# Moving token forms, attention steps, output transposes and a load in a two-layer trunk kernel

## The chip, the cores and the metric

The kernel runs on one core of a Trainium2 chip. The metric is the device time of one execution in microseconds, as the median of several executions. The profile is one further execution, taken by the hardware profiler; its times are in microseconds from the first instruction (the span). TensorE is called PE in it, VectorE DVE, ScalarE ACT, GpSimd POOL and SyncE SP.

## The reference, cut to what matters

One step of a trunk of two layers over 128 prompt tokens and 512 sample tokens (640 in all), width 2048, all in float32. Each layer normalises its input and modulates it with a scale and a shift, projects it, mixes, and projects back with a gated residual:

```
h  = rms_norm(x, g) * (1 + scale) + shift
layer 0:  mixers A (windowed attention) and B (gated short convolution)
layer 1:  cq, ck, cv, cg, dq, dk, dv, dg = split(h @ w_in)
          C: o = softmax(q1 k1) v - lambda * softmax(q2 k2) v, rms_norm per head, 4 heads, v of 256
          D: dense grouped-query attention, 8 heads on 2 keys
          out = concat(C * silu(cg), D * silu(dg)) @ w_out
x = x + gate * out
```

The keys and values of 256 cached tokens are put ahead of the sample's own. Outputs are the new x of both groups and the new keys and values.

## The kernel before, in words

**Layout.** The activations are held transposed: channels on the 128 partitions, the 640 tokens along the free dimension, in two halves of 320 (`HV`). A tile is 128 columns of a weight matrix times all 640 tokens. Every operand is split into a high and a low part (`split`, L212: ScalarE copies to the rounded type, L213, VectorE subtracts, L214), and a product is three matmuls: high by high, high by low, low by high (L248 to L250, and L510 to L512 for pairs).

**Tiles in `run_tiles` (L292).** A tile has 16 blocks of the contraction in four quarters; a quarter (`proj_q`, L241) does four blocks for each half, 24 matmuls. So a tile is 32 groups of three matmuls, 96 in all. The first tiles of a run are leading tiles: they go together, quarter by quarter, while `make_h` makes the activations that they need. Afterwards tiles go one at a time; weights are loaded five quarters and split three quarters ahead.

**Two queues of work beside the tiles.** `prep` holds what a finished tile still needs (a key's normalisation and rotation, for example), `attn` holds attention steps, or the making of token forms. Both are Python generators; a step is what lies between two yields. `slot` (L284) advances all of `prep` and one step of `attn`; it is called after each quarter. With `mid` (layer 1's attention stage only) a fifth step is taken between the two halves of the second quarter (L384 to L387). `release` (L269) advances attention until nothing in it still reads a tile that is about to be given away. The order of the lines is the order in which the work is asked for; the framework's scheduler places each engine's instructions by it and by when it takes them to be ready, and gives out buffers as they come free.

**Pairs in `run_pairs` (L419).** Two output tiles at once are computed by seven products of half the contraction and half the tokens instead of eight: `Q1`, `N5`, `P6`, `Q2`, `P7`, `Q3`, `P4`. Some use sums of weight blocks: N5 uses A21 + A22 (L450), P6 adds A11 (L453), Q2 uses A12. A11, A12 and A21 are loads of 512 KB into four buffers named `w8`; A22 is two ordinary quarters. Before the first pair they are asked for in the order A11, A12, A21, A22 (L498). There are three such starts: layer 0's output projection, layer 1's first input columns, layer 1's output projection.

**Forms.** The products also need sums of token blocks, the forms T: `make_form` (L1055) computes three sums and a difference of 320 columns each on VectorE (L1057 to L1060) and splits the 960 columns. In layer 1 `forms1` (L1297) makes eight of them from the modulated x (`x1`), which it first finishes on ScalarE (L1306). It is put on `attn` when `h1_maker` (L1268) makes block 8 (L1294); the blocks come in the order 0 to 3, 8 to 11, 4 to 7, 12 to 15 in the leading tiles, of which there are three. Form j waits until block j + 8 is made. `project` (L1111) runs the leading tiles, then the single tiles up to the sixth, then the pairs; it advances `attn` once after each leading tile's quarter and twice per quarter in the single tiles.

**Layer 1's attention stage.** For each head of C four tiles are projected: two queries and two keys. `k_gen` (L553) turns a key tile: it copies it out, transposes it, normalises and rotates it, yields twice, releases the old key, and transposes it back. With the second key the value comes and then attention: `diff_gen` (L1403) goes through five blocks of 128 queries in `score` (two score matrices into one buffer S, softmax), `groups` (transposes of the probabilities), `weigh` (times v, L1437 to L1439, then the norm over ACT, DVE, POOL and DVE, L1441 to L1448) and `out` (two transposes, L1454, and the gate). Each block's parts lie in successive steps: `out(u - 2)` and `score(u, 0)` and `groups(u - 1)` in one, `score(u, 1)` and `weigh(u - 1)` in the next. D's heads use `pair_gen` in the same manner.

Of the kernel before, what the change touches and what calls it, by code (L numbers as in the profile page):

```python
# [50 lines left out]
def trunk_kernel(ctx: ExitStack, tc: tile.TileContext, I: dict, O: dict):  # L51
# [189 lines left out]
    def proj_q(pp, part, qd, pos, halves=HV, alone=False, js=(0, 4)):  # L241
        wh, wl = part
        for half_i, sl in halves:
            ps = pp[half_i][:, 0:HALF]
            for j in range(*js):
# [3 lines left out]
                PE.matmul(ps, wh[:, i, :], lo[:, sl], start=False, stop=False)  # L249
                PE.matmul(ps, wl[:, i, :], hi[:, sl], start=False, stop=(j == js[1] - 1 if alone else (pos == 3 and j == 3)))  # L250

    def new_pp(i):

        if i == 2:
            t = pS.tile([P, 1024], F32, tag="S", name="Sp")
            return t[:, 0:512], t[:, 512:1024]
        return tuple(pproj.tile([P, 512], F32, tag=f"p{h}{i}", name=f"p{h}") for h in "ab")
# [23 lines left out]

    credit = [0.0]

    def slot(fill=None, rate=0.0):  # L284
        advance(prep, len(prep))
        advance(attn, 1)
        credit[0] += rate
        while credit[0] >= 1.0:
            next(fill, None)
            credit[0] -= 1.0  # L290

    def run_tiles(jobs, w_ap, make_h, fill=None, rate=0.0, ahead=None, order=(0, 1, 2, 3), before=None,  # L292
# [86 lines left out]
        for i in range(lead, len(jobs)):  # L379
            fn = jobs[i][1]  # L380
            pp = new_pp((i - lead) % 2)
            split_last = last is not None and i == len(jobs) - 1
            for qd in range(4):
                if mid and qd == 1:  # L384
                    proj_q(pp, parts[t], qd, qd, HV[:1])
                    advance(attn, 1)
                    proj_q(pp, parts[t], qd, qd, HV[1:])  # L387
                else:
                    proj_q(pp, parts[t], qd, qd, HV[:1] if split_last else HV)
                if before and qd == 0:  # L390
                    before(i)
                t += 1
                run_ahead(t)
                if pending and not prep:
                    n = pending.pop(0)
                    begin(jobs[n][1], pps[n])
                slot(fill, 0.0 if lp else rate)
            if split_last:
                first = last(pp, 0)
                next(first)  # L400
                for qd in range(4):
                    proj_q(pp, parts[t - 4 + qd], qd, qd, HV[1:])
                    next(first, None)
                for _ in last(pp, 1):
                    pass
                return
            drain(prep)
            if i >= lead + grace and pending:
                settle()
            if lp and not pending and not prep:  # L410
                lp.__exit__(None, None, None)
                lp = None
                if freed:
                    freed()
            begin(fn, pp)
# [3 lines left out]
    def run_pairs(cols, w_ap, mov, room, begin, out, tail):  # L419
# [75 lines left out]
            else:  # L495
                out(p, 1, 0, ps, None)

        for n in ("A11", "A12", "A21", "A22"):  # L498
            load(0, n)
        ahead(0)  # L500
        for i, (p, name) in enumerate(seq):
# [48 lines left out]
                                   op0=ALU.add, op1=ALU.mult)  # L550


    def k_gen(ap, pp, tag, src, gain, new_out, then=None):  # L553
        raw = ap.tile([P, 2, P], F32, tag="ctxk", name="ctxk", bufs=1)
        nc.sync.dma_start(raw, src.rearrange("(c p) d -> p c d", p=P))
        x = stage(ap, pp)
        yield
        ss = small.tile([P, 5], F32, tag="ss", name="ss")
        kg = ap.tile([P, 5, P], F32, tag="rp", name="kg", bufs=3)
        junk = ap.tile([P, P], F32, tag="junk", name="junk", bufs=1)  # L560
        for sample in (True, False):
            t = to_rows(cols_of(x), sample)
            for i, b in enumerate(range(4) if sample else (4,)):
                A.activation(junk, t[:, i * P:(i + 1) * P], AF.Square, accum_out=ss[:, b:b + 1])
            if sample:
                V.tensor_mul(kg[:, 0:4, :], t.rearrange("p (b f) -> p b f", b=4),
                             gain[:, None, :].to_broadcast([P, 4, P]))
            else:
                V.tensor_mul(kg[:, 4, :], t, gain)
        r = small.tile([P, 5], F32, tag="r", name="r")  # L570
        V.tensor_scalar(ss, ss, 1.0 / P, EPS, ALU.mult, ALU.add)
        G.tensor_tensor(r, ss, half[:, 0:5], op=ALU.pow)
        V.tensor_mul(kg, kg, r[:, :, None].to_broadcast([P, 5, P]))
        nc.gpsimd.dma_start(new_out, kg[:, 4, :])
        m1 = ap.tile([P, 4, P], F32, tag="rp", name="m1", bufs=3)
        m2 = ap.tile([P, 4, P], F32, tag="rp", name="m2", bufs=3)
        x = kg[:, 0:4, :].rearrange("p b (a h f) -> p (b a) h f", a=2, h=2)
        y = m1.rearrange("p b (a h f) -> p (b a) h f", a=2, h=2)
        z = m2.rearrange("p b (a h f) -> p (b a) h f", a=2, h=2)
        V.tensor_mul(y, x, cosR[:, :, None, :].to_broadcast([P, 8, 2, 32]))  # L580
        V.scalar_tensor_tensor(out=z[:, :, 0, :], in0=x[:, :, 1, :], scalar=-1.0, in1=sinR,
                               op0=ALU.mult, op1=ALU.mult)
        V.tensor_mul(z[:, :, 1, :], x[:, :, 0, :], sinR)
        V.tensor_add(m1, m1, m2)
        yield
        yield
        release(tag)
        hi, lo = (ap.tile([P, 896], F32R, tag=tag + t, name=tag + t) for t in "hl")
        st[tag] = (hi, lo)
        t = psT()  # L590
        for c in range(2):
            PE.transpose(t[:, c * P:(c + 1) * P], raw[:, c, :], ident)
        split(hi[:, 0:CTX], lo[:, 0:CTX], t[:, 0:CTX])
        t = to_rows(lambda b: m1[:, b, :], True)
        split(hi[:, CTX:CTX + NS], lo[:, CTX:CTX + NS], t)
        t = to_rows(lambda b: kg[:, b, :], False)
        split(hi[:, CTX + NS:CTX + NT], lo[:, CTX + NS:CTX + NT], t)
        if then:
            prep.append(then())
# [668 lines left out]
    def h1_maker(k, hv):  # L1268
# [21 lines left out]
        if len(hv) == 2 or hv[0][0] == 1:  # L1290
            if k < 8:
                nc.gpsimd.dma_start(hdram[k], ht[k][:, :, HV[HX[1]][1]])
            made.add(k)
        if k == 8:  # L1294
            attn.append(forms1())

    def forms1():  # L1297
# [105 lines left out]
    def diff_gen(ap, h, v, ks, qs, late):  # L1403
# [55 lines left out]
                V.tensor_mul(d, x, d)  # L1459

        for u in range(7):
            if u >= 2:
                out(u - 2)
            if u < 5:
                score(u, 0)
            if 1 <= u < 6:
                groups(u - 1)
            if u < 6:
                yield
            if u < 5:  # L1470
                score(u, 1)
            if 1 <= u < 6:
                weigh(u - 1)
            if u < 6:
                yield
# [44 lines left out]
    for n, h in enumerate(heads):  # L1520
        load, vgen = v_then(256, I["cache_c_v"][0, 0, h], (2 * h, 2 * h + 1), O["new_c_v"][0, 0, h], diff_then(n, h))
        for m in range(2):
            jobs.append((OD["cq"] + (m * 4 + h) * P, q_job(f"q{m}" + "ab"[n % 2], "c_q_norm")))
        for m in range(2):
            job = k_job(f"k{m}", I["cache_c_k"][0, 0, m, h], "c_k_norm", O["new_c_k"][0, 0, m, h], vgen if m else None)
            jobs.append((OD["ck"] + (m * 4 + h) * P, job if m else with_load(load, job)))
    for n in range(4):
        kv, q = n // 2, "ab"[n % 2]
# [107 lines left out]
```

## Time and profile before

| what | us |
|---|---|
| median of 3 runs | 2325.76 |
| lowest and highest | 2324.11 and 2326.21 |
| the profiled execution | 2328.41 |
| its span | 2326.6 |
| TensorE busy in the span | 2269.8 |

A profile row "line engine op names" has a line of the kernel, an engine, an operation, and the tiles by the program's names as out<-in. In the timeline two numbers stand ahead, start and duration; the bracket behind has the engine's idle time before and what ended it. A row "x6" merges six instructions in sequence. Rows of waits have the total, the count and the longest.

### The profile page before, as it was taken

What the parts mean: (1) busy time and instruction counts of PE and PEld (TensorE: products, weight loads), DVE (VectorE), ACT (ScalarE), POOL (GpSimd) and SP (SyncE); (2) the same over time, 40 slices, a digit from 0 to 9 for tenths busy, and PEclk for the clock granted to TensorE, in tenths of its full rate; (3) what the DMA queues carried; (4) which work ended last, traced back from release to release, by engine and by line L of the source; (5) the groups of instructions that cost most, each with busy time, mean ns of one, the idle gap of its engine ahead of it and who ended that gap; (6) DMA issues with size and microseconds to landing.
All of it is one profiled execution on the core that took longest, in us unless ns stands there. A gap on an engine that the chain in (4) does not pass through costs nothing.

```text
span 2326.6 us, 41104 instructions
## 1 busy us (share of the span) xinstructions
PE 2269.8 (98%) x15900; PEld 2182.8 (94%) x15900; DVE 1589.4 (68%) x2831; ACT 1094.9 (47%) x2304; POOL 159.9 (7%) x224
## 2 busy tenths in 40 slices
PE   7999999999999999999989999999999999999999
PEld 5889899999999999999989999999999999999999
DVE  4666878779779776887786664465565645557775
ACT  5325652443522222544654443465565676755443
POOL 1000000100000000000100001111101110000101
PEclk9999999999999999999999999999999999999999
DMA  9975446547367564954543335223223212138542
GB/s 315 294 250 161 152 125 207 154 134 216 115 210 221 179 191 128 296 152 126 172 147 96 119 111 160 71 60 98 78 62 100 67 53 64 60 105 270 178 136 61
DMA packets 380901, 342.90 MB, mean 147 GB/s; under 512 B 16403, under 2 KB 338417, under 8 KB 380193
## 3 DMA queue, kind: packets, MB, share of 16 engines
q1 hardware_dynamic: 366288, 296.00, 41.9%
q0 software_dynamic: 13696, 42.10, 5.3%
q8 instruction: 125, 2.05, 0.4%
q10 hardware_dynamic: 720, 2.16, 0.3%
q14 instruction: 72, 0.58, 0.1%
HBM read 301.27 MB, written 38.93 MB: 146 GB/s over the span
## 4 chain that ended last, share of the span: by engine, by line
PE 43%; DVE 6%; ACT 4%; issue 3%; DMA 2%; POOL 1%; SPq 0%; POOLq 0%; DVEq 0%; ACTq 0%
PE pq L512 7%; PE pq L511 7%; PE pq L510 7%; PE pb L249 3%; PE pb L248 3%; PE pb L250 3%; PE pa L248 2%; PE pa L249 2%; PE pa L250 2%; PE T L710 1%; PE S L722 1%; ACT qsw L610 1%; ACT p L696 1%; PE T L539 1%; PE S L724 1%
## 5 line engine op out<-in xcount | busy, mean ns | idle before, releaser
L213 ACT ACTIVATE wh<-raw 128x512 fp32r<-128x512 f32 (+1 forms) x456 | 273.6, 601 | 619.2 <-PE pb L249 516.2
L248 PE MATMUL pa<-h,wh 128*128 128x320 f32 x1456 | 464.4, 320 | 10.3 <-ACT h L1286 3.8
L214 DVE TENSOR_TENSOR wl<-raw,wh 128x512 fp32r<-128x512 f32 (+1 forms) x456 | 296.8, 652 | 244.3 <-ACT wh L213 213.0
L249 PE MATMUL pa<-h,wh 128*128 128x320 f32 x1456 | 453.6, 312 | 1.6 <-DVE h L1288 0.7
L248 PE MATMUL pb<-h,wh 128*128 128x320 f32 x1456 | 452.3, 311 | 0.5 <-ACT h L1286 0.5
L250 PE MATMUL pa<-h,wl 128*128 128x320 f32 x1456 | 452.5, 311 | 0.0
L250 PE MATMUL pb<-h,wl 128*128 128x320 f32 x1456 | 451.6, 310 | 0.0
L249 PE MATMUL pb<-h,wh 128*128 128x320 f32 x1456 | 450.8, 310 | 0.0
L191 DVE SCALAR_TENSOR_TENSOR acc<-adaw,sT,acc 128x1024 f32<-128x1024 f32 x240 | 300.6, 1282 | 0.0
L248 PEld LDWEIGHTS pa<-h,wh 128*128 128x128 f32 x1456 | 274.9, 189 | 26.2 <-issue 12.0
L249 PEld LDWEIGHTS pa<-h,wh 128*128 128x128 f32 x1456 | 275.1, 189 | 6.9 <-issue 3.3
L250 PEld LDWEIGHTS pa<-h,wl 128*128 128x128 f32 x1456 | 274.8, 189 | 2.1 <-issue 2.1
L248 PEld LDWEIGHTS pb<-h,wh 128*128 128x128 f32 x1456 | 273.6, 188 | 1.8 <-ACT h L1286 1.0
L249 PEld LDWEIGHTS pb<-h,wh 128*128 128x128 f32 x1456 | 273.8, 188 | 0.8 <-issue 0.8
L250 PEld LDWEIGHTS pb<-h,wl 128*128 128x128 f32 x1456 | 273.7, 188 | 0.0
L510 PE MATMUL pq<-h,wh 128*128 128x320 f32 x640 | 199.4, 312 | 2.4 <-ACT wh L213 2.4
L512 PE MATMUL pq<-h,wl 128*128 128x320 f32 x640 | 198.7, 310 | 1.7 <-DVE wl L214 1.7
L511 PE MATMUL pq<-h,wh 128*128 128x320 f32 x640 | 198.2, 310 | 0.0
L512 PE MATMUL pq<-T,wl 128*128 128x320 f32 x480 | 147.7, 308 | 0.2 <-DVE wl L214 0.2
L511 PE MATMUL pq<-T,wh 128*128 128x320 f32 x480 | 147.9, 308 | 0.0
L510 PE MATMUL pq<-T,wh 128*128 128x320 f32 x480 | 147.7, 308 | 0.1
L213 ACT ACTIVATE wh<-sx 128x512 fp32r<-128x512 f32 x120 | 75.2, 632 | 119.8 <-PE pq L511 76.9
(419 smaller groups left out, 4085.2 us busy)
## 6 DMA issues: line engine op xcount, KB each, us to landing
adaw<-in_ada_w SPq DMA_DIRECT2D x128, 512.0 KB, 4.3
raw<-in_ev_w_in SPq DMA_DIRECT2D x176, 256.0 KB, 3.3
raw<-in_od_w_in SPq DMA_DIRECT2D x160, 256.0 KB, 2.8
ada<-in_ada_w SPq DMA_DIRECT2D x32, 1024.0 KB, 8.2
w<-in_od_w_in SPq DMA_DIRECT2D x24, 512.0 KB, 3.8
yd<-y POOLq DMA_DIRECT2D x32, 320.0 KB, 3.1
yin<-yd SPq DMA_DIRECT2D x32, 320.0 KB, 4.3
w<-yd SPq DMA_DIRECT2D x32, 320.0 KB, 4.0
```

The source lines that it names most:

```text
L191: V.scalar_tensor_tensor(out=acc[c], in0=w, scalar=sT[:, kt, c:c + 1], in1=acc[c], op0=ALU.mult, op1=ALU.add)
L213: A.activation(hi, x, AF.Copy)
L214: V.tensor_sub(lo, x, hi)
L248: PE.matmul(ps, wh[:, i, :], hi[:, sl], start=(j == js[0] if alone else (pos == 0 and j == 0)), stop=False)
L249: PE.matmul(ps, wh[:, i, :], lo[:, sl], start=False, stop=False)
L250: PE.matmul(ps, wl[:, i, :], hi[:, sl], start=False, stop=(j == js[1] - 1 if alone else (pos == 3 and j == 3)))
L510: PE.matmul(ps, wh[:, j, :], hi, start=(new and h == 0 and j == 0), stop=False, **kw)
L511: PE.matmul(ps, wh[:, j, :], lo, start=False, stop=False, **kw)
L512: PE.matmul(ps, wl[:, j, :], hi, start=False, stop=(h == 1 and j == 3), **kw)
L539: PE.transpose(t[:, i * P:(i + 1) * P], src(b), ident)
L610: A.copy(sw[32 * d:32 * d + 32, :], x[32 * (d ^ 1):32 * (d ^ 1) + 32, 0:NS])
L696: A.activation(p[:, 0:n], s, AF.Exp, scale=rsc, bias=nm, accum_out=l)
```

## The change

Four edits, and what they need. `forms1` is put on `attn` when the last block (15) of the leading tiles is made, so all eight forms are asked for behind it: three after the leading tiles of the last quarter, the others in the slots of the first single tile. In the attention stage a tile's five attention steps are taken after 7, 13, 19, 26 and 32 of its 32 groups, and `slot` takes none there. In `diff_gen`, `out(u - 2)` moves behind the first yield, so it stands with `weigh(u - 1)`, and every one of the seven rounds yields once in its first part. The first key of each head of C yields once more before its release. And A21 is asked for ahead of A12 at the start of the pairs.

```diff
+    FIFTHS = (7, 13, 19, 26, 32)
+
+    def proj_parts(pp, part, qd):
+        wh, wl = part
+        n = 8 * qd
+        for half_i, sl in HV:
+            ps = pp[half_i][:, 0:HALF]
+            for j in range(4):
+                hi, lo = hs[qd * 4 + j]
+                PE.matmul(ps, wh[:, j, :], hi[:, sl], start=(qd == 0 and j == 0), stop=False)
+                PE.matmul(ps, wh[:, j, :], lo[:, sl], start=False, stop=False)
+                PE.matmul(ps, wl[:, j, :], hi[:, sl], start=False, stop=(qd == 3 and j == 3))
+                n += 1
+                yield n
...
-    def slot(fill=None, rate=0.0):
+    def slot(fill=None, rate=0.0, attend=True):
         advance(prep, len(prep))
-        advance(attn, 1)
+        if attend:
+            advance(attn, 1)
...
             for qd in range(4):
-                if mid and qd == 1:
-                    proj_q(pp, parts[t], qd, qd, HV[:1])
-                    advance(attn, 1)
-                    proj_q(pp, parts[t], qd, qd, HV[1:])
+                if mid:
+                    for n in proj_parts(pp, parts[t], qd):
+                        if n in FIFTHS:
+                            advance(attn, 1)
...
-                slot(fill, 0.0 if lp else rate)
+                slot(fill, 0.0 if lp else rate, not mid)
...
-        for n in ("A11", "A12", "A21", "A22"):
+        for n in ("A11", "A21", "A12", "A22"):
             load(0, n)
...
-    def k_gen(ap, pp, tag, src, gain, new_out, then=None):
+    def k_gen(ap, pp, tag, src, gain, new_out, then=None, more=0):
...
-        yield
-        yield
+        for _ in range(2 + more):
+            yield
         release(tag)
...
-        if k == 8:
+        if k == KT - 1 and hv[-1][0] == 1:
             attn.append(forms1())
...
         for u in range(7):
-            if u >= 2:
-                out(u - 2)
             if u < 5:
                 score(u, 0)
             if 1 <= u < 6:
                 groups(u - 1)
-            if u < 6:
-                yield
+            yield
+            if u >= 2:
+                out(u - 2)
             if u < 5:
                 score(u, 1)
...
-            job = k_job(f"k{m}", ..., vgen if m else None)
+            job = k_job(f"k{m}", ..., *((vgen,) if m else (None, 1)))
```

More of the change, by code (lines that the diff above doesn't have):

```diff
@@ L1524, in trunk_kernel @@
         for m in range(2):
-            job = k_job(f"k{m}", I["cache_c_k"][0, 0, m, h], "c_k_norm", O["new_c_k"][0, 0, m, h], vgen if m else None)
+            job = k_job(f"k{m}", I["cache_c_k"][0, 0, m, h], "c_k_norm", O["new_c_k"][0, 0, m, h], *((vgen,) if m else (None, 1)))
             jobs.append((OD["ck"] + (m * 4 + h) * P, job if m else with_load(load, job)))
```

## The prediction

> **What bounds the kernel now.** I read the page first, then the stages by windows, then TensorE's waits over the whole run, then single stretches of the timeline.
>
> ```profile
> span 2326.6 us, 41104 instructions
> ...
> PE 2269.8 (98%) x15900; PEld 2182.8 (94%) x15900; DVE 1589.4 (68%) x2831; ACT 1094.9 (47%) x2304; POOL 159.9 (7%) x224
> ```
>
> TensorE is busy for 98% of the span. The change adds and removes no matmul, so all that it can win or lose is TensorE's idle time. The page's busy time leaves 57 us of it; the windows say where (columns: the stretch, its length, then busy time and count of PE, PEld, DVE, ACT, POOL, granted clock, DMA share, GB/s):
>
> ```profile
> 1142.00:1195.00 53.00, 46.77 (x295) 44.48 (x295) 50.58 (x110) 42.59 (x86) 5.45 (x8) 0.97 0.59 174
> 1195.00:1237.00 42.00, 42.00 (x288) 42.00 (x288) 24.69 (x45) 16.26 (x31) 2.74 (x5) 1.00 0.37 115
> ...
> 2160.00:2175.00 15.00, 12.67 (x77) 12.11 (x76) 11.94 (x18) 7.06 (x15) 2.35 (x4) 0.89 0.80 237
> ```
>
> The three rows are the leading tiles of layer 1's input projection, the three single tiles behind them, and the first pair of the last projection. In the leading tiles VectorE is busy for 50.6 of 53 us and TensorE loses 6.2; in the next 42 us TensorE loses nothing and VectorE is free for 17. TensorE's waits, over the run (total, times, longest):
>
> ```profile
> PE T L1454 <- DVE on L1448: 5.7, 12, 0.9
> PE T L539 <- DVE m L584: 4.1, 4, 1.4
> PE pa L248 <- ACT h L1286: 3.8, 3, 1.6
> ...
> PE S L722 <- ACT p L696: 3.3, 7, 2.0
> PE pq L510 <- ACT wh L213: 2.4, 2, 1.4
> PE pq L512 <- DVE wl L214: 1.9, 4, 0.9
> PE T L1439 <- DVE ptl L214: 1.9, 4, 0.7
> ...
> PE pa L248 <- DVE kept L1333: 1.1, 1, 1.1
> PE pa L249 <- DVE h L1288: 0.7, 1, 0.7
> PE pb L248 <- ACT h L1286: 0.5, 1, 0.5
> ...
> PE T L771 <- DVE ptl L214: 0.9, 1, 0.9
> ```
>
> These idle times are too small, because a matmul's row is longer than its pitch:
>
> ```profile
> 2165.70 0.31 PE L512 MATMUL pq<-h,wl 128*128 128x320 f32 x1
> ...
> 2166.14 0.31 PE L512 MATMUL pq<-h,wl 128*128 128x320 f32 x1
> 2167.88 0.42 PE L510 MATMUL pq<-h,wh 128*128 128x320 f32 x1 [1.44 <-ACT wh L213]
> ...
> 2169.99 0.47 PE L510 MATMUL pq<-h,wh 128*128 128x320 f32 x1
> 2170.26 0.47 PE L511 MATMUL pq<-h,wh 128*128 128x320 f32 x1
> ```
>
> From 2165.70 to 2166.14 lie three pitches, so one is 0.147 us. From 2166.14 to 2167.88 pass 1.74 us: 1.59 more than a pitch, where the row shows 1.44 idle. So each wait costs about 0.15 us more than its row.
>
> **Part 1, outputs transposed later.** In differential attention `out` (L1451) transposes what `weigh` (L1431) made one step earlier. One such step:
>
> ```profile
> 1633.27 0.34 PE L724 MATMUL S<-k1h,q1bl 128*128 128x384 f32 x1
> ...
> 1634.00 0.95 DVE L689 TENSOR_REDUCE nm<-S 128x1 f32<-128x768 f32 x1
> ...
> 1634.98 0.30 ACT L691 ACTIVATE nm<-nm,rq1b 128x1 f32<-128x1 f32 x1 [0.84 <-DVE nm L689]
> ...
> 1635.31 0.99 ACT L696 ACTIVATE p<-S,nm,rq1b 128x768 f32<-128x768 f32 x1
> ...
> 1635.48 0.28 PE L1439 MATMUL T<-vh,ptl 128*128 128x256 f32 x1
> ...
> 1638.70 0.48 DVE L1448 SCALAR_TENSOR_TENSOR on<-on,rn,con 128x256 f32<-128x256 f32 x1 [0.74 <-POOL rn L1447]
> 1639.24 0.44 PE L1454 MATMUL T<-ident,on 128*128 128x128 f32 x2 [0.85 <-DVE on L1448]
> ...
> 1639.70 0.94 PE L710 MATMUL T<-ident,p 128*128 128x128 f32 x6
> ```
>
> The last matmul of `weigh` ends at 1635.76 and the normalised block at 1639.18: a chain of 3.4 us through ACT, DVE and POOL. TensorE had 12 projection matmuls (1.76 us) and half a score to do meanwhile, and stood. With the change the transposes come one step later, so another 18 to 21 matmuls (2.6 to 3.1 us), a score and a group of transposes lie between; that covers the chain with over 3 us to spare. All 12 waits should go: 5.7 + 12 x 0.15 = 7.5 us at most, and nothing at least, if TensorE meets its next wait sooner. I take 7.0, near the rows. It costs one step more per head (13 yields for 12, so 14 advances with the last). Head h+1's k0 must not be released before that: `more=1` puts its release behind the 15th advance; without it a step would run unspaced. The k0 job's 11 transposes and three splits move one quarter later, to the slot ahead of k1's staging. They hide under a quarter of matmuls (24 x 0.147 = 3.5 us); if not, at most their wait on m, at 1.4 the longest, returns four times. No step that moves here issues a load; the two saves of y on POOL's queue leave one step later, and nothing reads them before the gate tiles that end the stage.
>
> **Part 2, even steps.** Before, a tile's five steps follow 8, 4, 4, 8 and 8 of its 32 groups of three matmuls, so two gaps are 1.76 us and three 3.5 us. After, the gaps are 6 or 7 groups, 2.6 to 3.1 us. What the short gaps cost are waits for split probabilities (1.9 + 0.9 idle, five waits: 3.6 with what rows hide), and parts of the waits on p (3.3) and m (4.1), some of which stand in layer 0, untouched. These are bounds of 0 and some 7 us; I take 3.0, the value of the rows that name a short gap.
>
> **Part 3, the pair's loads.** The second product of a pair (N5) adds A21 and A22; A21 was loaded third.
>
> ```profile
> 977.25 1.01 SPq L426 DMA_DIRECT2D w<-in_ev_w_out  x2
> ...
> 980.13 0.44 SPq L426 DMA_DIRECT2D w<-in_ev_w_out  x1
> 987.39 1.29 DVE L450 TENSOR_TENSOR sx<-w,raw 128x512 f32<-128x512 f32 x2 [1.83 <-DMA w<-in_ev_w_out]
> ...
> 2155.11 1.19 SPq L426 DMA_DIRECT2D w<-in_od_w_out  x2
> 2161.63 0.37 SPq L426 DMA_DIRECT2D w<-in_od_w_out  x1
> 2166.47 1.29 DVE L450 TENSOR_TENSOR sx<-w,raw 128x512 f32<-128x512 f32 x2 [1.65 <-DMA w<-in_od_w_out]
> ...
> w<-in_od_w_out SPq DMA_DIRECT2D x1, 512.0 KB, 6.2
> ```
>
> Two loads leave together; the third waits for a buffer and leaves 2.4 and 5.3 us after the second. The last row is the second load alone, 6.2 us to landing, so at 2162.1 to 2162.5 instead of 2166.5. As second, A21 gains about 2.4 and 4 us. TensorE's waits there are pq's: 2.4 + 1.9 + 6 x 0.15 = 5.2 us. A12 becomes third; it serves the fourth product, two products (7 us) later than N5, and would have to slip by more than that to be felt. At the third such place, layer 1's input projection, the row from 1195 to 1237 shows no idle time to win.
>
> After the last wait the matmuls run at a pitch of 0.27 (2169.99 to 2170.26), and the clock of that stretch is 0.89. Twelve such matmuls lose 12 x 0.12 = 1.4 us. The Trainium skill, TensorE: Matmul & The Clock Gate, "Part 1: The HAM clock gate", says that TensorE falls to half speed after an idle window of about 3.4 us and rises after a busy one; 0.27 against 0.147 agrees roughly with half. By that rule the 1.4 us go entirely with the waits; without it they would stay. Bounds from rows are 0 and 5.2 + 1.4 = 6.6; I take 5.5, since the rows show waits on one load alone, and a little may be left of splits behind the addition.
>
> **Part 4, the forms.** Eight forms are made in layer 1, each of four 320-column operations and a 960-column split on VectorE:
>
> ```profile
> L214 DVE TENSOR_TENSOR wl<-raw,wh 128x512 fp32r<-128x512 f32 x16 | 10.9, 693 | 2.1 <-ACT wh L213 2.1
> L214 DVE TENSOR_TENSOR T<-sx,T 128x960 fp32r<-128x960 f32 x8 | 9.3, 1160 | 0.7 <-ACT T L213 0.7
> ...
> L1057 DVE TENSOR_TENSOR sx<-T,w 128x320 f32<-128x320 f32 x4 | 2.0, 494 | 0.0
> ```
>
> One form takes 4 x 0.49 + 1.16 = 3.1 us. Seven ran among the leading tiles: 22 of VectorE's 50.6 us, while TensorE waited for h. Without them VectorE has some 29 us of work there beside 288 x 0.147 = 42.3 us of matmuls. The waits there (3.8 + 1.1 + 0.7 + 0.5, and 6 x 0.15) are 7.0 us, the bound above; I take 5.0, since the first quarter after the split halves still supplies h only just in time. The forms land on the last leading quarter (three) and on the first single tile (five), 25 us of VectorE in a stretch with 10 us of the last quarter and 17 free behind it. Queued behind a form on VectorE are the splits of weights, made three quarters (10.6 us) ahead, and the gates that free the banks; neither is due before a form is over. A lower bound below nothing is the third rival. Moved with the forms is no DMA, but the loads of the first pair wait for buffers that the first four forms free, which are due only behind three tiles (42 us).
>
> **Sum.** 7.0 + 3.0 + 5.5 + 5.0 = 20.5, less 2 us for waits which come next: 18.5. The profiled execution took 2328.4 us, so 2309.9; it stands 2.65 above the median of 2325.76, which gives 2307 for a median.
>
> **Rivals.** (1) Half only: the stalls are one queue's lateness, and each one removed makes the next longer. For it: DVE stands on the chain of most waits. Against: the waits lie far apart, in stages with free time between them. 9 us: 2317. (2) Written order is not issued order.
>
> ```profile
> 1134.84 0.72 PE L1238 MATMUL T<-ones,sq 128*128 128x1 f32 x6
> ```
>
> This row of six matmuls of the norm stands between the L510 and the L511 of one quarter of products, where no line puts them, so instructions are placed by something other than the lines. Then parts 1 and 2 move little, parts 3 and 4 stay: 10.5 less 2: 2317. (3) The forms' chain: `sx` has one buffer, so a form is 1.96 + ScalarE's half (no row above; taken as long as VectorE's 1.16) + 1.16, about 4.3 us, and eight take 34 us behind the last h; if the first gates queue behind three of them, single tiles wait for banks and part 4 gives back its 5: 2312. The same page ("Architectural detail") says that ACT and DVE take instructions strictly in order, which is this rival's condition; the 0.7 us of idle in the split's row is all that the trace shows of it. (4) Slower: evening the gaps uncovers the softmax. S has one buffer; from the end of the score the chain reduce, negate, exp takes 2.7 us (about 1633.6, the end of L724's row, to 1636.3, the end of L696's). The step behind `score(u, 0)` has 0.7 us of transposes (1639.70 to 1640.4) and now 2.6 of matmuls: 3.3. If splits ahead of it on VectorE (0.69 each) lengthen the chain beyond 3.3, the three long gaps of five, which covered it, no longer do. There are 40 such steps; from 18.5 / 40 = 0.46 us each they eat the gain, and at 0.6 they cost 24: 2325.8 - 18.5 + 24 = 2331. Against: with gaps of 1.76 the same wait is only 3.3 us in the whole run.
>
> **Chances.** Forecast (2298 to 2313) 0.60; half 0.19; written order 0.06; forms' chain 0.06; slower 0.09. A measurement tells about 0.2% (4.7 us) from no change. Faster takes the first, the fourth, and most of the second and third: 0.86; within 0.2% 0.05; slower 0.09. The low end is all bounds taken, 7.5 + 7 + 6.6 + 7 = 28 below the median: 2298; the high end takes in the halves: 2320. About 0.81 lie between.
>
> **What would show it.** Right: no wait of T L1454 on L1448 above 0.2; L450's addition freed by 2163 or earlier with no wait of pq behind it, and a clock of 1.00 there; the stretch of the leading tiles some 5 us shorter, with VectorE's busy share high behind it instead of in it; ptl's waits below 1 us. Wrong: waits of S L722 above 10 us, waits of pa on `kept` or on wl in the single tiles behind the leading ones, or the T L1454 waits unchanged.

## The result, and the profile after

The changed kernel takes 2299.18 us (median of 4 runs, 2296.36 to 2299.24), the kernel before beside it 2325.80 (4 runs, 2324.11 to 2326.21): a ratio of 0.9884, 95% interval 0.9867 to 0.9901, or 26.6 us less. The forecast was 2307.0 in a range of 2298 to 2320. Its direction and its places were right; it was 8 us short.

The page of the changed kernel, its span and its busy times:

```profile
span 2294.5 us, 41094 instructions
...
PE 2255.1 (98%) x15900; PEld 2178.4 (95%) x15900; DVE 1590.6 (69%) x2831; ACT 1089.8 (47%) x2304; POOL 160.5 (7%) x224
```

No engine's number of instructions changed. TensorE's busy time fell by 14.7 us, since a matmul's row contains part of a short stand, so it is no measure of work here. The three stretches which the prediction showed, in the changed kernel (stretch, length, busy time and count of PE, PEld, DVE, ACT, POOL, granted clock, DMA share, GB/s):

```profile
1135.00:1180.00 45.00, 44.63 (x293) 44.39 (x294) 42.92 (x97) 38.75 (x83) 6.47 (x10) 0.96 0.64 188
1180.00:1222.00 42.00, 41.61 (x284) 41.35 (x283) 33.10 (x59) 18.94 (x35) 2.17 (x4) 1.00 0.48 149
2128.00:2143.00 15.00, 14.61 (x102) 14.06 (x101) 13.62 (x24) 8.16 (x18) 2.87 (x5) 1.00 0.94 272
```

The leading tiles pass in 45 instead of 53 us. VectorE is still busy for 95% of them (42.9 of 45, where it was 50.6 of 53): the stretch became as much shorter as VectorE's work in it. The single tiles behind took up the difference (33.1 for 24.7) and hide it. The pair's stretch has its full clock. TensorE's waits over the run (total, times, longest); lines past the new function are 15 or 16 higher than before, so L1470 is L1454, L738 is L722, L526 is L510:

```profile
PE T L555 <- DVE m L600: 4.8, 4, 1.6
PE pa L248 <- ACT h L213: 2.3, 3, 1.4
...
PE S L738 <- ACT p L712: 1.8, 3, 1.4
...
PE T L634 <- DVE ptl L214: 1.5, 3, 0.6
...
PE T L1470 <- DVE on L1464: 0.7, 1, 0.7
...
PE T L787 <- DVE ptl L214: 0.5, 1, 0.5
...
PE pq L526 <- ACT wh L213: 0.3, 1, 0.3
...
PE pq L528 <- DVE wl L214: 0.2, 1, 0.2
```

The waits for h out of L1286 and L1288 (now L1302, L1304) and for `kept` are gone altogether, eleven of the twelve on `on` too, and those of the pair's products came down from 4.3 to 0.5. Here is why, for one `out`, in the changed kernel's timeline:

```profile
1636.95 0.28 PE L1455 MATMUL T<-vh,ptl 128*128 128x256 f32 x1
1637.28 0.47 ACT L1457 ACTIVATE on<-T,rl 128x256 f32<-128x256 f32 x1 [0.96 <-PE T L1455]
...
1639.27 0.48 DVE L1464 SCALAR_TENSOR_TENSOR on<-on,rn,con 128x256 f32<-128x256 f32 x1 [0.73 <-POOL rn L1463]
...
1643.68 0.44 PE L1470 MATMUL T<-ident,on 128*128 128x128 f32 x2
```

The normalised block is ready at 1639.75, 2.8 us after the start of the last matmul of `weigh`; its transposes now come at 1643.68, 3.9 us later still.

**Where the time went.** Both kernels run the same projection matmuls, in the same order but for some 90 places inside layer 1's leading tiles. So time can be compared between the n-th and the m-th of the 320-column matmuls of the two traces. All profiles of this study, in us:

| profile | first 1152 | layer 0's first pairs, 5184 to 5472 | layer 1's leading tiles, 6400 to 6816 | attention stage, 8640 to 11232 | layer 1's output, start, 11232 to 11616 |
|---|---|---|---|---|---|
| before | 234.0 | 46.4 | 69.5 | 626.3 | 64.1 |
| changed | 227.9 | 47.5 | 61.2 | 611.7 | 60.7 |
| after_again | 229.3 | 44.8 | 61.3 | 611.6 | 60.7 |
| forms_alone | 228.0 | 47.7 | 61.2 | 626.1 | 65.8 |
| load_alone | 229.5 | 45.1 | 69.5 | 625.7 | 61.1 |
| out_alone | 229.0 | 48.9 | 69.5 | 620.9 | 66.4 |
| even_alone | 229.0 | 47.0 | 69.5 | 623.8 | 62.0 |
| not_even | 228.5 | 46.1 | 61.6 | 621.3 | 62.0 |
| not_out | 229.1 | 44.2 | 61.2 | 623.7 | 61.0 |
| crowded | 228.5 | 44.8 | 61.2 | 626.6 | 61.0 |
| forms_half | 231.3 | 45.2 | 67.0 | 612.0 | 64.4 |
| no_more | 230.1 | 45.3 | 61.3 | 612.3 | 61.2 |

What isn't listed differs by less than 1.9 us between any two of them. In the second column the changed kernel is 1.1 us slower: it gains 2.2 in the pair itself, but loses 3.2 ahead of it, where its clock was 0.89 (950 to 965 us) and that of before 1.00. From before to changed the leading tiles gained 8.3, the attention stage 14.7 and the output's start 3.4. The first column is no part of the change: up to layer 0's first pair, about 983 us in, TensorE has the same instructions in the same order. The 6.1 us by which the shown profile of before is slower there are its own. They are why the spans differ by 32.1 and the medians by 26.6.

### The profile page after: what moved, and what is told of

Its sections match the earlier page's. It is cut to its first block, busy times and chain, and to the rows that moved or that the text cites. A ratio compares the mean times of both kernels' runs of the same rounds, so it can differ in the third digit from the quotient of the medians.

```text
span 2294.5 us, 41094 instructions
## 1 busy us (share of the span) xinstructions
PE 2255.1 (98%) x15900; PEld 2178.4 (95%) x15900; DVE 1590.6 (69%) x2831; ACT 1089.8 (47%) x2304; POOL 160.5 (7%) x224
## 3 DMA queue, kind: packets, MB, share of 16 engines
q1 hardware_dynamic: 366288, 296.00, 42.9%
## 4 chain that ended last, share of the span: by engine, by line
PE 84%; DVE 5%; ACT 4%; issue 3%; DMA 3%; POOL 1%; SPq 0%; POOLq 0%; ACTq 0%; DVEq 0%
PE pq L528 7%; PE pq L527 7%; PE pq L526 7%; PE pa L248 6%; PE pb L248 6%; PE pa L249 6%; PE pb L249 6%; PE pa L250 6%; PE pb L250 6%; PE pb L262 2%; PE pb L261 2%; PE pa L261 2%; PE pb L263 2%; PE pa L263 2%; PE pa L262 2%
## 5 line engine op out<-in xcount | busy, mean ns | idle before, releaser
L248 PE MATMUL pa<-h,wh 128*128 128x320 f32 x1024 | 326.0, 319 | 3.7 <-ACT h L213 2.3
L249 PE MATMUL pa<-h,wh 128*128 128x320 f32 x1024 | 319.2, 313 | 1.1 <-DVE h L214 1.0
L250 PE MATMUL pa<-h,wl 128*128 128x320 f32 x1024 | 318.7, 311 | 0.4 <-DVE wl L214 0.4
L249 PE MATMUL pb<-h,wh 128*128 128x320 f32 x1024 | 317.8, 310 | 0.0
L248 PE MATMUL pb<-h,wh 128*128 128x320 f32 x1024 | 317.6, 310 | 0.0
L250 PE MATMUL pb<-h,wl 128*128 128x320 f32 x1024 | 317.5, 310 | 0.0
L248 PEld LDWEIGHTS pa<-h,wh 128*128 128x128 f32 x1024 | 193.1, 189 | 17.8 <-issue 10.4
L526 PE MATMUL pq<-h,wh 128*128 128x320 f32 x640 | 199.0, 311 | 0.3 <-ACT wh L213 0.3
L249 PEld LDWEIGHTS pa<-h,wh 128*128 128x128 f32 x1024 | 193.3, 189 | 6.2 <-issue 3.3
L250 PEld LDWEIGHTS pa<-h,wl 128*128 128x128 f32 x1024 | 193.2, 189 | 2.7 <-issue 2.1
L249 PEld LDWEIGHTS pb<-h,wh 128*128 128x128 f32 x1024 | 192.6, 188 | 0.8 <-issue 0.8
L248 PEld LDWEIGHTS pb<-h,wh 128*128 128x128 f32 x1024 | 192.5, 188 | 0.7 <-issue 0.4
L250 PEld LDWEIGHTS pb<-h,wl 128*128 128x128 f32 x1024 | 192.6, 188 | 0.0
L526 PE MATMUL pq<-T,wh 128*128 128x320 f32 x480 | 147.8, 308 | 0.1
L261 PE MATMUL pa<-h,wh 128*128 128x320 f32 x432 | 141.2, 327 | 0.0
```

Of the source, the lines that this page charges most:

```text
L248: PE.matmul(ps, wh[:, i, :], hi[:, sl], start=(j == js[0] if alone else (pos == 0 and j == 0)), stop=False)
L261: PE.matmul(ps, wh[:, j, :], hi[:, sl], start=(qd == 0 and j == 0), stop=False)
L526: PE.matmul(ps, wh[:, j, :], hi, start=(new and h == 0 and j == 0), stop=False, **kw)
```

## The experiments

The theory was that the four edits act where the prediction put them, each on its own waits, so that single edits add up. The rivals: that attention's two edits cover or uncover each other's waits; that the edits of attention don't follow the written order; and, for the forms, that it is a load or a bank and not VectorE which holds the leading tiles. First, each edit alone.

**forms_alone**: only the place where `forms1` is put on the queue.

```diff
-        if k == 8:
+        if k == KT - 1 and hv[-1][0] == 1:
             attn.append(forms1())
```

> The kernel before, with the forms of layer 1 asked for behind the last leading block and nothing else. Theory A (the parts stand in separate stretches and add up): this part is worth what the two profiles differ by between the start of the leading tiles and the end of the first single tile, 8 us: 2318 (2316 to 2320), TensorE's waits on h (L1286, L1288) and on kept gone. Theory B (the stages share one lateness, so a part alone is worth less than in company): at most 4 us: 2322. Theory C (the forms only move the stall into the single tiles): 2325, with waits on wl or kept behind the leading tiles.

Measured: 2314.73 us (2313.87 to 2317.22) against 2325.41, ratio 0.9956 (0.9941 to 0.9971), 10.7 less. The leading tiles take 61.2 us, as in the whole change, so this gain, 8.3 us by the table, depends on nothing else.

**load_alone**: only the order of the pair's loads.

```diff
-        for n in ("A11", "A12", "A21", "A22"):
+        for n in ("A11", "A21", "A12", "A22"):
```

> The kernel before, with A21 asked for ahead of A12 at the start of the pairs and nothing else. Theory A: the two starts that waited for A21 lose their waits, 3 us in layer 0's output and 3.4 in layer 1's: 2319.5 (2318 to 2321), and the second stretch keeps a clock of 1.00. Theory B: less than 3 us, above 2322.5, because in company with the other parts the last projection starts at another point of its loads. If only layer 1's start gains, 2322.

Measured: 2319.96 us (2317.27 to 2323.36), ratio 0.9980 (0.9971 to 0.9990), 5.5 less. By the table the output's start takes 61.1 instead of 64.1. These two columns vary by some us from profile to profile, so all profiles are used: with the new order (eight) layer 0's first pairs have a mean of 45.4 and layer 1's start one of 61.5, without it (four) 47.5 and 64.6. That is 2.2 and 3.1 us, 5.2 before rounding, but single profiles overlap (47.5 with the new order and 46.4 without it; 64.4 and 62.0). Most of the spread lies ahead of the pairs. From the pair's own first matmul, the 5376th, to the 5472nd all eight profiles with the new order take 15.4 or 15.5 us and the four without it 16.6 to 17.6. From the 11568th to the 11616th it is 8.4 to 9.1 in seven and 11.7 in forms_half, against 10.1 to 12.8. The means differ by 1.7 and 2.6, so 4.3 us. A part of the 2.6 is the clock: it is halved there in three of the four profiles without the new order (not in even_alone, the 10.1) and in one of the eight with it, forms_half, where one wait of 1.9 is left.

**out_alone**: only the outputs one step later, with the extra yield.

```diff
         for u in range(7):
-            if u >= 2:
-                out(u - 2)
...
-            if u < 6:
-                yield
+            yield
+            if u >= 2:
+                out(u - 2)
```

> The kernel before, with the output transposes one step later and the additional yield of the first key, but the attention steps spaced as before. Theory A: the 12 waits of the transposes on L1448 go, 7 us, and what remains of the 15 us of the attention stage needs the even steps: 2318.8 (2317 to 2320.5), waits on ptl (L1439) still 2 us. Theory B2 (one of the two suffices, since both give the chain more time): 12 us or more: 2314 or less. Theory D (later transposes without even steps run into the next short gap): 2323 or more, with the waits moved to ptl or S.

Measured: 2319.88 us (2315.35 to 2322.38), ratio 0.9969 (0.9959 to 0.9978), 5.5 less; the attention stage takes 620.9, 5.4 less. All waits on `on` are gone, but others have come. TensorE's waits inside the attention stage, out_alone:

```profile
PE T L1437 <- DVE ptl L214: 2.8, 3, 0.9
...
PE T L1439 <- DVE ptl L214: 0.7, 1, 0.7
```

In before, TensorE's listed waits on ptl in this loop were four at L1439, 1.9 us in all. Here they are four again, but 3.5 us. Each lies at a head's last block, the only one whose step has no score between the transposes of p and `weigh`. The split that it waits for stands on VectorE behind the next head's key, kg times r, and that one waits for GpSimd. VectorE in before, at the second head:

```profile
1664.62 0.82 DVE L573 TENSOR_TENSOR kg<-kg,r 128x640 f32<-128x640 f32 x1 [0.68 <-POOL r L572]
1665.36 0.28 DVE L214 TENSOR_TENSOR ptl<-T,pth 128x128 fp32r<-128x128 f32 x1
```

and the same place in out_alone:

```profile
1657.22 0.28 ACT L213 ACTIVATE pth<-T 128x128 fp32r<-128x128 f32 x1 [0.74 <-PE T L710]
...
1658.43 0.83 DVE L573 TENSOR_TENSOR kg<-kg,r 128x640 f32<-128x640 f32 x1 [1.35 <-POOL r L572]
...
1659.17 0.28 DVE L214 TENSOR_TENSOR ptl<-T,pth 128x128 fp32r<-128x128 f32 x1
...
1659.51 0.39 PE L1437 MATMUL T<-vh,pth 128*128 128x256 f32 x1 [0.93 <-DVE ptl L214]
```

The high part is ready at 1657.50, while VectorE stands idle for GpSimd; still the split begins only at 1659.17, behind kg. So the wait comes from the place of the step beside the key's work, and not from the gap's length alone.

**even_alone**: only `proj_parts`, the five places, and `slot` without its step.

```diff
-                if mid and qd == 1:
-                    proj_q(pp, parts[t], qd, qd, HV[:1])
-                    advance(attn, 1)
-                    proj_q(pp, parts[t], qd, qd, HV[1:])
+                if mid:
+                    for n in proj_parts(pp, parts[t], qd):
+                        if n in FIFTHS:
+                            advance(attn, 1)
```

> The kernel before, with the five attention steps of a tile a fifth apart, and the output transposes where they were. Theory A: 15 - 7 = 8 us from waits on ptl and from S: 2318 (2316 to 2320), the waits on L1448 still there in number, over 4 us. Theory B2: the even gaps (2.6 us at least, where 1.76 was) cover most of the 3.4 us chain together with a score, so the waits on L1448 fall below 3 us and it is worth 12 us or more: 2314 or less. My record's step took 3 us for the even steps: 2323.

Measured: 2318.22 us (2316.38 to 2323.85), ratio 0.9974 (0.9962 to 0.9986), 7.2 less; the attention stage takes 623.8, 2.6 less. TensorE's waits in that stage, even_alone:

```profile
PE T L1470 <- DVE on L1464: 8.1, 12, 1.0
...
PE T L634 <- DVE ptl L214: 1.5, 3, 0.6
```

The waits of `weigh` on ptl are gone: at the last block the transpose of p (1652.98) now comes ahead of the key's transposes (1653.68), where in before it came behind them (1663.32 and 1660.06). But the waits of the transposes of `on` rose from 5.7 to 8.1 us. Block by block, before and here: behind each head's first block they are 0.19 to 0.25 us, then 0.53 to 0.59, since 18 projection matmuls stand there instead of 24; behind the second 0.84 to 0.88, then about 0.4 in three heads and 0.87 in one; behind the last 0.32 to 0.45, then 0.92 to 0.95, which is most of the rise. VectorE at such a last block, even_alone:

```profile
1659.14 0.69 DVE L596 TENSOR_TENSOR m<-kg,tables 128x512 f32<-128x512 f32 x1
...
1660.42 0.15 DVE L1461 TENSOR_SCALAR ssq<-ssq 128x1 f32<-128x1 f32 x1
...
1661.68 0.48 DVE L1464 SCALAR_TENSOR_TENSOR on<-on,rn,con 128x256 f32<-128x256 f32 x1
```

The last matmul of `weigh` starts at 1657.05 and ends at about 1657.3; the block is normalised at 1662.16, 4.8 us later and not 3.4, since VectorE first rotates the next head's key. The 27 projection matmuls of about 4.0 us that stand between don't cover that.

The median lies where theory A put it (2318), but in the stage, the only one that the edit touches, the gain is 2.6, near the prediction's 3.0.

So out and even gain 5.4 and 2.6 in their stage alone, 8.0 in all, and 14.7 together. The next two took each of them away from the whole change.

**not_even**: the changed kernel with the old places of the steps (even_alone's edit backwards).

> The changed kernel with the attention steps spaced as before (8, 12, 16, 24, 32 groups); the other three edits stay. In the profiles the stretch of layer 1's attention (from the start of its second single tile to the start of the 27th) takes 626.4 us before, 620.9 with the later transposes alone, 623.8 with the even steps alone, and 611.7 with both. Theory I (the two edits need each other: either alone moves the wait that it removes into the other's): 620.9 here, 9 us more than with both, so about 2308 (2306 to 2311), with waits on ptl back at 2 us or more. Theory A (they add up; the medians of the runs with one part alone sum to 28, the whole change is worth 27): 6 us more: 2305 (2303 to 2306).

Measured: 2306.75 us (2305.57 to 2308.74), ratio 0.9928 (0.9913 to 0.9943); the stage takes 621.3.

**not_out**: the changed kernel with the outputs at their old place (out_alone's edit backwards).

> The changed kernel with the output transposes where they were (and no additional yield of the first key); forms, load and even steps stay. Theory I: the attention stretch takes 623.8 as with even steps alone, 12 us more than with both: 2311 (2309 to 2314), waits of the transposes on L1448 at about 8 us. Theory A: 7 us more: 2306 (2304 to 2308).

Measured: 2309.60 us (2307.33 to 2313.88), ratio 0.9945 (0.9927 to 0.9964); the stage takes 623.7.

Both stand where the edits alone put them (620.9 and 623.8) and 9.7 and 12.1 us above the changed kernel's 611.7. The medians alone would not have shown this: the four single gains sum to 28.9 by them, with intervals of 4 to 7 us each. The stages show it: the two edits need one another. The 6.7 us that are more than the sum come for the most part from the waits which each edit alone brings, as the fences of waits show: 8.1 on `on` for 5.7 without the one, 3.5 on ptl in `weigh` for 1.9 without the other, and with both 0.7 and none. By the distances of matmuls from start to start, each against the median of its width, `on` accounts for 2.7 and `weigh` for 3.2 of the 6.7; the rest is spread.

**crowded**: the changed kernel with the steps close together at the beginning of each tile.

```diff
-    FIFTHS = (7, 13, 19, 26, 32)
+    FIFTHS = (3, 6, 9, 12, 15)
```

> The changed kernel with the five steps after 3, 6, 9, 12 and 15 groups of a tile: gaps of 1.32 us and then 17 groups (7.5 us) of plain matmuls. The work is the same. Theory G (what counts is the time between a step and the next; the softmax chain of 2.7 us and the chain behind weigh of 3.4 us are uncovered by 1.3 us of matmuls): waits on p (S) and ptl, 40 steps of each kind and some 0.5 us each: 20 to 40 us more, 2320 to 2340. Theory W (the order that is issued is made by readiness, whatever the written positions): within 5 us of the changed kernel, 2295 to 2304.

Measured: 2310.83 us (2310.11 to 2311.12), ratio 0.9944 (0.9929 to 0.9959). Neither expectation held: it is 13.0 less than before beside it, where the whole change gives 26.6. The stage takes 626.6, all of the 14.7 us given back, but no more. TensorE's waits in the attention stage, crowded:

```profile
PE T L634 <- DVE ptl L214: 2.9, 4, 0.7
PE T L555 <- DVE m L600: 2.7, 5, 1.4
PE T L786 <- ACT pth L213: 1.7, 4, 0.5
PE S L738 <- ACT p L712: 1.6, 4, 0.5
PE T L787 <- DVE ptl L214: 0.8, 1, 0.8
```

and in the changed kernel:

```profile
PE T L555 <- DVE m L600: 2.2, 2, 1.4
PE T L634 <- DVE ptl L214: 1.5, 3, 0.6
...
PE T L787 <- DVE ptl L214: 0.5, 1, 0.5
...
PE S L738 <- ACT p L712: 0.4, 2, 0.2
```

All the listed waits of the stage come to 10.9 us in crowded and 6.7 in the changed kernel, 4.2 of 15. Both have the same 4255 matmuls in this stretch. If one takes them from start to start, and counts what each distance has above the median of its width, crowded has 15.0 us more. It is spread: 3.4 ahead of the score matmuls L738, the ones that wait for p; 3.2 ahead of the queries' sums of squares, L634; 2.9 ahead of the products with pth in D's heads, L786; 2.5 ahead of the transposes of p, L726; 1.2 ahead of L1470; and the rest in small distances, many of which the waits' view doesn't list. So distance between the steps is worth 15 us, but no one resource takes it, and the softmax takes at most 3.4 of it.

**forms_half**: the changed kernel with the forms put on the queue at block 4, half way between the old and the new place.

```diff
-        if k == KT - 1 and hv[-1][0] == 1:
+        if k == 4:
```

> The changed kernel with the forms asked for when the third of the four groups of leading blocks begins (block 4), between where they were (block 8) and where the change has them (block 15). Three forms then stand in the third quarter of the leading tiles and three in the fourth. Theory V (VectorE's supply of h is what the leading tiles wait for, and each form ahead of an h delays it by 3.1 us, less the slack): some 3 to 6 of the 8.3 us come back, 2302 to 2305, waits on h (L1302, L1304) of 2 to 4 us. Theory K (it is the gates and banks at the end of the leading tiles, which only depend on the forms' being over): no loss or a gain, 2297 to 2300, since the forms are over earlier.

Measured: 2303.65 us (2301.21 to 2306.65), ratio 0.9914 (0.9898 to 0.9930), 20.1 less than before beside it, where the whole change gives 26.6: theory V. The leading tiles take 67.0 us, between 61.2 and 69.5. First its leading tiles' window, then TensorE's waits there:

```profile
1137.00:1187.00 50.00, 46.19 (x289) 44.19 (x288) 47.11 (x102) 41.34 (x85) 4.56 (x7) 0.95 0.63 182
```

```profile
PE pa L248 <- DVE kept L1349: 1.8, 1, 1.8
PE pa L248 <- ACT h L1302: 1.3, 2, 1.0
PE pa L249 <- DVE h L1304: 0.7, 1, 0.7
```

VectorE's work in the leading tiles is 50.6, 47.1 and 42.9 us in before, forms_half and the changed kernel, the windows 53, 50 and 45 us long: VectorE is at 94 or 95% in each, and the stretch is as long as its work. That dose and its answer speak for VectorE's work as the cause, and not for a load. The 1.8 on `kept` is a wait for a bank, but for one that VectorE (L1349) empties late. Nor does TensorE's own speed set the stretch: in load_alone its clock fell inside the leading tiles, and they still took the 69.5 us of before. From 1155 to 1170 us, load_alone:

```profile
1155.00:1170.00 15.00, 12.27 (x70) 11.46 (x69) 15.00 (x30) 11.40 (x23) 2.06 (x3) 0.89 0.72 209
```

VectorE is busy all the time; the clock of before is 1.00 in the same window.

**no_more**: the changed kernel without the extra yield of the first keys.

```diff
-            job = k_job(f"k{m}", I["cache_c_k"][0, 0, m, h], "c_k_norm", O["new_c_k"][0, 0, m, h], *((vgen,) if m else (None, 1)))
+            job = k_job(f"k{m}", I["cache_c_k"][0, 0, m, h], "c_k_norm", O["new_c_k"][0, 0, m, h], vgen if m else None)
```

> The changed kernel without its one extra yield in the keys of cache_c_k (loop of two yields instead of three). Everything else as changed. Such a key then takes its two buffers a quarter tile (about 3.6 us) sooner, and taking them first runs out, without matmuls between, whatever steps of the earlier head's attention task still hold that key. Theory R (the extra yield is needed because the task has one step more since the outputs come later): at the three later heads that have a predecessor, one or two steps fall together at the quarter's end; waits of the transposes L1470 on L1464, or of S on p, of 0.8 to 2 us come back there, the attention stage (projection matmuls 8640 to 11232) takes 613.5 to 617 us instead of 611.7, the time is 2301 to 2305. Theory N (the extra yield is without weight, the sixth step of each tile is never outstanding at that point): the stage stays within 0.7 us of 611.7, the waits on m grow by at most 3 us in all, and the time is within 3 us of the changed kernel's run beside it.

Measured: 2298.67 us (2297.67 to 2299.91) against 2324.88, ratio 0.9888 (0.9872 to 0.9905). The stage takes 612.3, 0.6 more, and the waits on m are 4.1 instead of 4.8: theory N. In its sequence of matmuls the last two transposes of `on` of a head do fall ahead of the next key's, unspaced, as feared; at that place their block has long been ready, and TensorE doesn't wait. It costs at most the 0.6 us.

**after_again**: the changed kernel once more.

> The changed kernel once more, unaltered, beside the other on one chip. Theory G: the gain is the sum of the stages that the single edits moved (forms 8.3, attention 14.7, layer 1's output loads 3, in all 26), so against the kernel before the ratio is 0.987 to 0.990, and the profile has 61.3 us from matmul 6400 to 6816, 611.7 from 8640 to 11232 and about 61 from 11232 to 11616. Theory P: about 5 of the 32 us between the two profiles lie ahead of the first changed instruction and are of the one execution; a second profile of the changed kernel then has again 228 to 231 us in the first stretch, where the kernel before had 234.0 in its shown profile, or, if the difference were of the kernel, the runs of the variants would not have had 228 to 231 too. If the gain is otherwise, the stage times differ by over 2 us from these.

Measured: 2297.27 us (2295.20 to 2298.42) against 2324.88 (2322.82 to 2326.28), ratio 0.9880 (0.9866 to 0.9895). The stages repeat to 0.1 us in the three that the change moves; the first stretch has 229.3. So both expectations held. No experiment points to a version that is faster than the changed kernel.

## Why the prediction was right, and where it was off

**Bound.** Right. The gain is idle time of TensorE, in the leading tiles, the attention stage and the starts of the pairs, where the prediction's rows of waits lay. That the sum of 26.6 stayed inside the range is in part luck: its low end took 28 for all bounds, two of which were passed (parts 1 and 2 together, 14.7 for 14.5, and part 4, 8.3 for 7.0), while part 3 stayed below its own of 6.6.

**Part 1 and part 2** (7.0 and 3.0; measured together 14.7). In the whole change the waits went as foreseen: those on `on` (5.7 to 0.7), ptl's in `weigh`, and in the step shown the chain is covered with 3.9 us to spare. The step that failed is the sum of the two parts, as if each acted on waits of its own. Alone they are worth 5.4 and 2.6, close to the 7.0 and 3.0 that were taken; together they are worth 6.7 more, above both parts' taken values though about at the sum of their upper bounds (14.5). Two readings lie behind it. The chain behind `weigh` was read in one step, as 3.4 us; at a head's last block even_alone shows 4.8, behind the next key's rotation. The prediction knew that evening turns gaps of 3.5 into 2.6 to 3.1; it used that for the softmax, as a rival, and not for `on`, which is where even_alone shows it. And the waits on ptl in `weigh` were put down to the short gap; the rows show the key's product ahead of the split on VectorE, and the even steps help by bringing the transposes of p ahead of the key's.

**Part 3** (5.5; measured 4.3 in the pairs themselves, 5.2 in the columns of the table). About right in size. What would show it came out only in part. The order of the adding in the changed kernel's timeline:

```profile
2126.55 1.19 SPq L442 DMA_DIRECT2D w<-in_od_w_out  x2
...
2132.67 0.37 SPq L442 DMA_DIRECT2D w<-in_od_w_out  x1
...
2133.57 1.22 DVE L471 TENSOR_TENSOR sf<-w,w 128x1024 f32<-128x1024 f32 x1
...
2136.76 1.28 DVE L466 TENSOR_TENSOR sx<-w,raw 128x512 f32<-128x512 f32 x2
...
2138.16 0.42 PE L526 MATMUL pq<-h,wh 128*128 128x320 f32 x1 [0.35 <-ACT wh L213]
```

A21 now leaves with the first load, and the addition no longer waits for it: the bracket of 1.65 behind the load is gone. But the time at which it starts, set against the matmuls around it (28.6 us earlier than in before), is only 1.1 us better, not the 3.5 that were said. VectorE is now what is late: it has no idle time there, and it takes `sf` (A11 + A21, which the lines ask for later) ahead of the sum for the second product. A wait of 0.35 is left. The clock is 1.00, as said: the 1.4 us of matmuls at half rate went with the waits, and here the trace agrees with the rule that the prediction weighed. It isn't so in every run: in forms_half a wait of 1.9 was left, and the clock from 2140 to 2165 was 0.93.

**Part 4** (5.0; measured 8.3). The term that was mis-sized. The upper bound of 7.0 was the listed waits and 0.15 for each of six; from start to start these stands are 8.5 us in before, at eight places, and all of it went but 0.2. The doubt about the first quarter, for which 2 us were kept back, was unfounded. The count of forms was wrong as well: not seven but five of the splits lay ahead of 1195 in before (1162.35 the first, 1192.11 the fifth), and two start ahead of 1180 now. VectorE lost 7.7 us of work there, not 22, and remained at 95%, where the text had foreseen it free. VectorE sets the pace there (15.00 of 15.00 us busy from 1155 to 1170 in before), so about each us of its work that leaves is a us of the stretch: 7.7 us of work, 8 of time.

**Less 2 us for waits that come next.** New waits did come, about as large as that: 1.5 us on ptl ahead of L634 in D's heads, so ptl's waits are not below 1 us in all, and 0.4 on wl in the single tiles, which the prediction had named as a sign of being wrong. But the stages' gains are counted with them, so the reduction only added to the shortfall. The four terms, 20.5, were lower than the stages' 27 or so because of parts 1, 2 and 4.

**The rivals.** Half only: no, the two edits of attention did the opposite. Written order: its condition is met on VectorE (`sf` ahead of the sum that is written before it), but the transposes and the steps moved as written. The forms' chain: the changed kernel's eight splits run from 1175 to 1212, 37 us, near the 34 that were worked out, yet no tile waited for a bank; the single tiles lose 0.4 of 42 us. The softmax: S's waits on p in the attention stage fell from 1.3 to 0.4, so 3.3 us of cover are enough for a chain of 2.7; with steps of three groups (crowded) it does show, as at most 3.4 us of 15.

## What to carry to other kernels

Two edits that act on the same loop are to be worked out together: write down, for each chain in the loop, its length and the time between its two ends with the one edit, the other and both, and do so at every block, since here the last block of a head had the longest chain. Where an engine is at 95% over a whole stretch, take the stretch to be as long as that engine's work; here the waits listed for TensorE (6.1 us) fell short of the 8.3 that went. And compare profiles from one matmul to the same matmul, stage by stage, since here 6 us of the two spans' difference lay in instructions that were the same.

## What the runs showed of the hardware that was not expected

**The same instructions took 227.9 to 234.0 us** in the first stretch over twelve profiles, up to 6 us or 0.3% of the run. Part of it is the clock. The two slowest are before, with two stretches there in which the granted clock is below 1.00, and forms_half (231.3), with one; the other ten have none. Before:

```profile
150.00:170.00 20.00, 17.65 (x147) 15.14 (x147) 10.95 (x30) 5.27 (x13) 0.60 (x1) 0.91 0.63 218
240.00:250.00 10.00, 8.02 (x48) 7.45 (x47) 9.09 (x17) 7.95 (x17) 0.00 (x0) 0.83 0.65 204
```

What brings them about in one execution and not in another stays open.

**Half rate came without a wholly idle stretch.** Before's timeline at the pair, beside the rows of the prediction:

```profile
2169.56 0.64 PE L512 MATMUL pq<-h,wl 128*128 128x320 f32 x1 [0.90 <-DVE wl L214]
...
2172.39 0.76 PE L539 MATMUL T<-ident,xr 128*128 128x128 f32 x3
2172.89 0.41 PE L510 MATMUL pq<-h,wh 128*128 128x320 f32 x1
```

From the last matmul ahead of the stands (2166.14) to this one TensorE stood for 1.6 and 1.1 us and did four matmuls between. From 2169.56 on the pitch was 0.27, until about 2172.9, and 0.147 after that. The Trainium skill, TensorE: Matmul & The Clock Gate, "Part 1: The HAM clock gate", gives about 3.4 us for the window, and the 3.3 us at half rate agree; but the stretch before it was not idle, only for about 2.7 of 3.4 us, so a rule by which only a gap longer than the window counts would have missed it.
